# Keeping the last expert's rows on chip and adding them with TensorE

## The chip, the cores and the metric

The kernel runs on one core of a Trainium2 chip. The metric is the device time of one execution in microseconds (us). The core's engines are named as the profile names them: PE is TensorE (PEld its weight loads), ACT is ScalarE, DVE is VectorE, POOL is GpSimd, and SP is SyncE, which here issues most of the loads. Each engine works through its own queue of instructions in order; DMA queues move data between device memory (DRAM tensors, names ending in `_d`) and the chip. PSUM is the memory that TensorE writes into, 8 banks of 128 rows by 512 fp32 numbers.

## The reference, cut to what matters

The program computes two transformer blocks on 1024 tokens of width 1024. The first ends in a mixture of experts; the second begins with a norm of the result and a projection. In between:

```python
# end of block 1: x_tok [1024 tokens, 1024], 16 experts, each takes its 128 best tokens
logits = x_tok @ w_router;  aff = softmax(logits)
g, idx = top_k(aff.T, 128)                       # gate and token index of each expert's rows
xs = x_tok[idx]                                  # [16, 128, 1024]
y = (silu(xs @ w_gate) * (xs @ w_up)) @ w_down * g[..., None]
ff = zeros([1024, 1024]).at[idx].add(y)          # a token may be taken by several experts
h = h + g2 * rmsnorm(ff, norm_post_ffn)
# start of block 2
u = rmsnorm(h, norm_w)
proj = u @ w_in                                  # 8 column groups, then the HGRN and the
...                                              # forgetting-attention branches, output, final norm
```

Products are made in about fp32 precision: each factor is split into a high and a low part (type fp32r) and three products hi·hi, hi·lo and lo·hi are summed (`mm3`, L78 to L84).

## The kernel before, in words

**Order of the work.** The functions issue operations in program order into a tile framework. A planner then puts each engine's operations into one fixed queue, by the times at which it expects them to be ready; among ready ones, program order decides. Memory on chip and PSUM are handed out in pools, stacked and opened and closed by the program; a tile of a later pool may lie on the bytes of an earlier one, and then waits for the last use of the tiles it lies on.

**The experts (`moe`, L679).** The loop runs 17 times. Pass e multiplies the 128 rows of expert e by its gate and up weights (`rows` into the PSUM tiles pg and pu) and, in the same pass, expert e-1's hidden rows by its down weights (py). Weights come in pieces of 1 MB: SP loads a piece into one of 6 slots `raw` (L535), ACT casts it to `whi` (L87), and DVE takes the difference to `wlo` (L88). At the end of a pass ACT applies silu (L713, tile `sl`), DVE multiplies by pu (L714, tile `hh`), and `combine` (L772) finishes expert e-1: ACT multiplies py by the gate into `y` (L776), and POOL issues an indirect DMA (L777) that adds the 128 rows of y at their tokens into `ff_d` in device memory. `chosen` fetches the next expert's rows `xs` by an indirect DMA. The last pass, e = 16, holds only the down product and combine of expert 15.

**Block 1's end and block 2's start (`ffn_out`, L793).** For each of 8 blocks of 128 tokens SP loads the residual `h` (L803) and the experts' sum `ff` (L805), 512 KB each. ACT squares ff with a running sum (L808), the reciprocal root comes from a logarithm and an exponential (L92, L93), DVE scales ff (L810) and adds it to h (L811); h is stored, squared again (L813), and its reciprocal root is put on a diagonal `dg` (L816). After each 4 blocks (a group), for each of 8 column slices k, TensorE multiplies h by dg, which transposes and scales (L822, PSUM tile `tp`, 2 buffers); ACT makes `uh` (L824) and DVE `ul` (L825), the split transposed input of block 2.

**What follows (`hgrn`).** `wk` (L828) loads the first columns of block 2's weights, `raw` with 2 buffers (load L835, 512 KB in 512-byte pieces), and splits them; `chan` (L863) multiplies them with uh and ul into PSUM tiles `mm`, by L82 to L84. The mm and the tp tiles belong to one PSUM pool, `b2p` (L789), which holds both `ffn_out` and `hgrn`. `hgrn` reads its `masks` last at L1058 and ends with transposes (L1139) and stores (L1141, L1181). Then the attention stage opens pools on the same bytes and banks; its first load on SP, `cmask` (L1196), reads an input of the program.

Of the kernel before, what the change touches and what calls it, by code (L numbers as in the profile page):

```python
# [40 lines left out]
def f(ap):  # L41
    return ap.bitcast(F32)
# [7 lines left out]
class Kernel:  # L50
# [628 lines left out]
    def moe(self):  # L679

        with ExitStack() as st:
# [3 lines left out]
            pp = self.pool(st, "moep", 1, space=PSUM)  # L685
            xs = self.chosen(0, w, pp)
            hh = None
            for e in range(NE + 1):
# [20 lines left out]
                if e < NE:  # L709
                    hh = self.t(w, [P, D], F32, "hh", bufs=2)  # L710
                    for n in range(2):
                        sl = self.t(w, [P, 512], F32, "sl", bufs=2)
                        self.silu = self.nc.scalar.activation(sl, pg[n], AF.Silu)  # L713
                        self.nc.vector.tensor_tensor(hh[:, n * 512:(n + 1) * 512], sl, pu[n], op=ALU.mult)  # L714
                if e:
                    self.combine(e - 1, w, py)
        self.stx.close()
# [53 lines left out]

    def combine(self, e, w, py):  # L772

        y = self.t(w, [P, D], F32, "y", bufs=2)
# [5 lines left out]
    def block2(self):  # L780
        with ExitStack() as st:
            self.stu = ExitStack()
            up = self.pool(self.stu, "uT", side="right")
            self.u = [(self.t(up, [P, KB, 512], F32R, f"uh{g}"), self.t(up, [P, KB, 512], F32R, f"ul{g}")) for g in range(2)]
            self.pj = self.pool(st, "pj")
            self.jobs, self.ready = [], []
            with ExitStack() as st2:
                self.pp = self.pool(st2, "b2p", 2, space=PSUM)
                self.ffn_out()  # L789
                self.hgrn()  # L790
            self.fox()

    def ffn_out(self):  # L793

        nc, pp = self.nc, self.pp
        with ExitStack() as st:
            w = self.pool(st, "fo")
            for g in range(2):
                us = []
                for b in range(4):  # L800
                    r = slice((g * 4 + b) * P, (g * 4 + b + 1) * P)
                    h = self.t(w, [P, D], F32, "h", bufs=8)
                    nc.sync.dma_start(h, self.h_d[r, :])  # L803
                    ff = self.t(w, [P, D], F32, "ff", bufs=4)
                    nc.sync.dma_start(ff, self.ff_d[r, :])  # L805
                    sq = self.t(w, [P, D], F32, "sq", bufs=2)
                    ss = self.t(w, [P, 2], F32, "ss", bufs=4)
                    nc.scalar.activation(sq, ff, AF.Square, accum_out=ss[:, 0:1])  # L808
                    self.rstd(ss[:, 0:1], D)
                    nc.vector.scalar_tensor_tensor(ff, ff, ss[:, 0:1], self.G2, op0=ALU.mult, op1=ALU.mult)  # L810
# [4 lines left out]
                    dg = self.t(w, [P, P], F32, "dg", bufs=8)  # L815
                    nc.vector.tensor_scalar(dg, self.ident, ss[:, 1:2], None, op0=ALU.mult)  # L816
                    us.append((h, dg))
                uh, ul = self.u[g]
                for k in range(KB):
                    tp = self.t(pp, [P, 512], F32, "tp", bufs=2)  # L820
# [3 lines left out]
                    nc.scalar.activation(uh[:, k, :], tp, AF.Copy, scale=nw)  # L824
                    nc.vector.scalar_tensor_tensor(ul[:, k, :], tp, nw, f(uh[:, k, :]), op0=ALU.mult, op1=ALU.subtract)  # L825
# [36 lines left out]

    def chan(self, ws, g, m=P):  # L863

        ps = self.t(self.pp, [P, 512], F32, "mm", bufs=self.nmm)
        x = self.u[g]
        self.mm3(ps[:m, :], [(ws[k], (x[0][:, k, :], x[1][:, k, :])) for k in range(KB)])
        return ps

    def toks(self, ws, b):  # L870

        ps = self.t(self.pp, [P, 512], F32, "mm", bufs=self.nmm)
        for j in range(2):
            x, t0 = self.u[(b + j) // 4], ((b + j) % 4) * P
            self.mm3(ps[:, j * 256:(j + 1) * 256], [((x[0][:, k, t0:t0 + P], x[1][:, k, t0:t0 + P]), ws[k]) for k in range(KB)])
# [614 lines left out]
def shape_constants():  # L1490
# [14 lines left out]
        "k_ident": np.eye(P, dtype=np.float32),  # L1505
        "k_cos": np.ascontiguousarray(np.concatenate([cos, cos], 0)),
# [28 lines left out]
```

## Time and profile before

| | us |
|---|---|
| median of 3 runs (lowest, highest) | 2838.47 (2833.11, 2840.96) |
| the profiled execution | 2839.24 |
| its span | 2837.3 |
| idle of PE between the last expert and block 2 | 24.65 |
| the last expert's scatter, start to landing | 10.50 |

The profiled execution is one run with the hardware profiler on; its span is the time from its first to its last instruction, and all stretches below are microseconds from the start of that span. Mean granted clock of TensorE over the span: 0.966 of full. In a timeline row the columns are start, duration, engine and line, operation with output<-input, shapes and how many in a row; in brackets the idle time of the engine before it and what ended it. A chain of waits follows the work that ended last backwards, each piece with its start, duration and engine.

### The profile page before, as it was taken

The page shows a single profiled execution, that of the slowest core. Times are in us where ns is not written, and L with a number is a line of the kernel's source. Part 1 is how long each engine was busy: PE and PEld are TensorE (multiplying, and loading weights), DVE is VectorE, ACT ScalarE, POOL GpSimd, SP SyncE. Part 2 cuts the span into 40 slices and gives each one's busy share as a digit, 9 for nine tenths or more (in the row PEclk, how much of TensorE's full clock was granted, in tenths as well). Part 3 has the DMA queues.
Part 4 walks back from the last instruction along what each step waited for, and adds up shares of the span by engine and source line. Part 5 has one row for each costly group of instructions (what it writes and reads, how often), then busy time and mean ns, then how long its engine had stood idle before and what let it go on. Part 6 is the DMA issues. An engine that isn't in the chain of part 4 may idle for free.

```text
span 2837.3 us, 38733 instructions
## 1 busy us (share of the span) xinstructions
PE 2638.5 (93%) x14237; PEld 2221.2 (78%) x14237; DVE 1995.0 (70%) x3298; ACT 1620.8 (57%) x2858; POOL 247.6 (9%) x355
## 2 busy tenths in 40 slices
PE   6999999899799999997699999998999998989998
PEld 3777888777588877776589999997878787777886
DVE  5965899844798888886656777763777676786535
ACT  4212898833477777775644555543666665674335
POOL 0101000000300000000100000000111111230000
PEclk8999999999899999999799999999999999999999
DMA  7665332256599999997612122336665666465612
GB/s 274 221 229 191 102 91 88 86 178 211 216 390 381 366 370 375 377 362 234 233 39 46 45 46 38 46 81 164 175 166 133 156 163 135 141 194 188 207 60 82
DMA packets 306018, 516.44 MB, mean 182 GB/s; under 512 B 52529, under 2 KB 180094, under 8 KB 304804
## 3 DMA queue, kind: packets, MB, share of 16 engines
q1 hardware_dynamic: 288556, 456.04, 50.8%
q0 software_dynamic: 11136, 36.25, 4.3%
q10 hardware_dynamic: 6136, 21.67, 2.0%
q8 instruction: 113, 1.85, 0.3%
q14 instruction: 77, 0.63, 0.1%
HBM read 421.01 MB, written 92.88 MB: 181 GB/s over the span
## 4 chain that ended last, share of the span: by engine, by line
PE 72%; DMA 10%; ACT 8%; DVE 6%; issue 3%; SPq 1%; POOL 0%; DVEq 0%; ACTq 0%; POOLq 0%
PE mm L82 13%; PE mm L84 12%; PE mm L83 12%; PE av L1333 2%; PE pu L763 2%; PE pu L764 2%; PE pu L762 2%; PE py L764 2%; PE py L763 2%; PE py L762 2%; PE pg L763 2%; PE pg L764 2%; PE sc L1052 2%; PE pg L762 2%; PE tp L1324 1%
## 5 line engine op out<-in xcount | busy, mean ns | idle before, releaser
L88 DVE TENSOR_TENSOR wlo<-raw,whi 128x2048 fp32r<-128x2048 f32 (+1 forms) x280 | 541.9, 1963 | 172.2 <-ACT whi L87 167.6
L87 ACT CAST whi<-raw 128x2048 fp32r<-128x2048 f32 (+1 forms) x284 | 459.6, 1656 | 137.1 <-PE mm L83 63.8
L82 PE MATMUL mm<-uh,whi 128*128 128x512 f32 x640 | 257.9, 403 | 0.9 <-ACT uh L824 0.9
L83 PE MATMUL mm<-ul,whi 128*128 128x512 f32 x640 | 255.0, 398 | 0.0
L84 PE MATMUL mm<-uh,wlo 128*128 128x512 f32 x640 | 254.4, 398 | 0.0
L84 PE MATMUL mm<-whi,ul 128*128 128x256 f32 x768 | 221.5, 288 | 0.0
L82 PE MATMUL mm<-whi,uh 128*128 128x256 f32 x768 | 221.1, 288 | 0.0
L83 PE MATMUL mm<-wlo,uh 128*128 128x256 f32 x768 | 218.8, 285 | 0.0
L84 PEld LDWEIGHTS mm<-whi,ul 128*128 128x128 f32 x768 | 148.1, 193 | 0.1
L82 PEld LDWEIGHTS mm<-whi,uh 128*128 128x128 f32 x768 | 148.0, 193 | 0.2
L83 PEld LDWEIGHTS mm<-wlo,uh 128*128 128x128 f32 x768 | 147.9, 193 | 0.2
L1302 ACT ACTIVATE lg<-lg,sm 128x128 f32<-128x128 f32 (+7 forms) x128 | 99.5, 777 | 80.4 <-DVE sm L1301 79.7
L84 PEld LDWEIGHTS mm<-uh,wlo 128*128 128x128 f32 x640 | 122.6, 192 | 24.4
L82 PEld LDWEIGHTS mm<-uh,whi 128*128 128x128 f32 x640 | 122.8, 192 | 23.3 <-ACT uh L824 1.4
L446 ACT ACTIVATE e<-sc,mx 128x512 f32<-128x512 f32 (+1 forms) x192 | 117.8, 624 | 40.4 <-DVE mx L445 39.6
L83 PEld LDWEIGHTS mm<-ul,whi 128*128 128x128 f32 x640 | 122.7, 192 | 22.0
L1333 PE MATMUL av<-pT,V 128*128 128x256 f32 x640 | 110.2, 300 | 19.8 <-ACT pT L87 15.1
L82 PE MATMUL mm<-xh,whi 128*128 128x512 f32 x320 | 126.8, 396 | 1.4 <-DVE cy L520 1.0
L84 PE MATMUL mm<-xh,wlo 128*128 128x512 f32 x320 | 126.4, 396 | 0.5 <-DVE wlo L88 0.5
L1333 PEld LDWEIGHTS av<-pT,V 128*128 128x128 f32 x640 | 93.3, 198 | 42.8 <-ACT pT L87 31.9
L83 PE MATMUL mm<-xl,whi 128*128 128x512 f32 x320 | 126.5, 395 | 0.0
L1298 DVE SCALAR_TENSOR_TENSOR lg<-sc,FT,nF 128x512 f32<-128x512 f32 (+3 forms) x160 | 91.7, 583 | 37.8 <-PE sc L1295 27.0
(392 smaller groups left out, 7002.1 us busy)
## 6 DMA issues: line engine op xcount, KB each, us to landing
raw<-in_w_gate_dram SPq DMA_DIRECT2D x64, 1024.0 KB
raw<-in_w_up_dram SPq DMA_DIRECT2D x64, 1024.0 KB
raw<-in_w_down_dram SPq DMA_DIRECT2D x64, 1024.0 KB
raw<-in_w_in_dram SPq DMA_DIRECT2D x76, 512.0 KB
wada<-in_w_ada_dram SPq DMA_DIRECT2D x32, 512.0 KB
Q<-Q_d SPq DMA_DIRECT2D x64, 256.0 KB
yraw<-yT_d SPq DMA_DIRECT2D x22, 512.0 KB
wa<-in_w_ada_dram SPq DMA_DIRECT2D x8, 1024.0 KB
```

The lines of the kernel that those rows point to most:

```text
L82: self.nc.tensor.matmul(ps, ah, bh, start=(i == 0), stop=False)
L83: self.nc.tensor.matmul(ps, ah, bl, start=False, stop=False)
L84: self.nc.tensor.matmul(ps, al, bh, start=False, stop=(i == n - 1))
L87: self.nc.scalar.copy(hi, src)
L88: (eng or self.nc.vector).tensor_tensor(lo, src, f(hi), op=ALU.subtract)
L446: nc.scalar.activation(e[:, c0:c0 + n], ps[:, :n], AF.Exp, scale=-1.0, bias=mx[:, m, c:c + 1], accum_out=sm[:, m, c:c + 1])
L762: self.nc.tensor.matmul(ps[n], xh[:, i, :], hi[:, k, c], start=(i == 0), stop=False)
L763: self.nc.tensor.matmul(ps[n], xh[:, i, :], lo[:, k, c], start=False, stop=False)
L764: self.nc.tensor.matmul(ps[n], xl[:, i, :], hi[:, k, c], start=False, stop=(i == KB - 1))
L1298: nc.vector.scalar_tensor_tensor(lg[:, c0:c0 + full], ps[:, :full], Ft, nF[:, c0:c0 + full], op0=ALU.subtract, op1=ALU.add)
L1302: nc.scalar.activation(lg[:, :n], lg[:, :n], AF.Exp, scale=-1.0, bias=sm[:, 0:1], accum_out=sm[:, 1:2])
L1333: nc.tensor.matmul(ps[:, :256], V[:, k, :], pT[k // 4][j][:, k % 4, :], start=(k + j == 0), stop=(k == nkb - 1 and j == 1))
```

## The change

The last expert (15) has no scatter any more. Its gated rows stay on chip as a high part `yh` (ACT) and a low part `yl` (DVE). While it runs, `places` builds a matrix `oh` [128 rows, 1024 tokens]: it loads a row 0..1023 on all partitions and compares it with the expert's token indices, 1 where equal. In `ffn_out` TensorE adds up, for each token block and each half of the columns, identity times ff (what the other 15 experts left in device memory) and oh times yh and yl, in PSUM; the square and the scaling read that sum. All 8 loads of h and all 8 of ff are issued ahead of the loop, into buffers of their own. `ffn_out` has a PSUM pool of its own, `fop` (the sums 3 x 2 banks, tp 2 banks: all 8), closed before `b2p` is opened for `hgrn`. uh and ul lie in the buffers that held the experts' weights (`mw`), which stays open. To make room, `hh`, `sl` and `y` have one buffer instead of two.

```diff
@@ -683,6 +683,11 @@
             self.pad(st, 64)
             self.ml = self.pool(st, "ml", 2)
             pp = self.pool(st, "moep", 1, space=PSUM)
+            self.stl = ExitStack()
+            lp = self.pool(self.stl, "last", side="right")
+            self.yh, self.yl = [self.t(lp, [P, D], F32R, x) for x in ("yh", "yl")]
+            self.oh = self.t(lp, [P, SEQ], F32R, "oh")
+            self.ix = self.t(lp, [P, 1], F32, "ix")
             xs = self.chosen(0, w, pp)
             hh = None
             for e in range(NE + 1):
@@ -707,14 +712,22 @@
                     for q in range(4):
                         self.rows(py, hT, q)
                 if e < NE:
-                    hh = self.t(w, [P, D], F32, "hh", bufs=2)
+                    hh = self.t(w, [P, D], F32, "hh", bufs=1)
                     for n in range(2):
-                        sl = self.t(w, [P, 512], F32, "sl", bufs=2)
+                        sl = self.t(w, [P, 512], F32, "sl", bufs=1)
                         self.silu = self.nc.scalar.activation(sl, pg[n], AF.Silu)
                         self.nc.vector.tensor_tensor(hh[:, n * 512:(n + 1) * 512], sl, pu[n], op=ALU.mult)
-                if e:
+                if e == NE - 1:
+                    self.places(e, w)
+                if e == NE:
+                    gate = self.gT[:, e - 1:e]
+                    for n in range(2):
+                        c = slice(n * 512, (n + 1) * 512)
+                        self.nc.scalar.activation(self.yh[:, c], py[n], AF.Copy, scale=gate)
+                        self.nc.vector.scalar_tensor_tensor(self.yl[:, c], py[n], gate, f(self.yh[:, c]), op0=ALU.mult, op1=ALU.subtract)
+                elif e:
                     self.combine(e - 1, w, py)
-        self.stx.close()
+        self.stu = self.stx
 
     def tsplit(self, pp, w, src, nblk, name, bufs=2):
 
@@ -769,9 +782,17 @@
         self.nc.gpsimd.indirect_dma_start(out=xs, out_offset=None, in_=self.xn2_d, in_offset=bass.IndirectOffsetOnAxis(ap=self.idxT[:, e:e + 1], axis=0))
         return self.tsplit(pp, w, xs, KB, "xs", bufs=2)
 
+    def places(self, e, w):
+
+        nc = self.nc
+        at = self.t(w, [P, D], F32, "xs", bufs=2)
+        nc.sync.dma_start(at, rowbc(self.I["k_iota"]))
+        nc.vector.tensor_copy(self.ix, self.idxT[:, e:e + 1])
+        nc.vector.tensor_scalar(self.oh, at, self.ix, None, op0=ALU.is_equal)
+
     def combine(self, e, w, py):
 
-        y = self.t(w, [P, D], F32, "y", bufs=2)
+        y = self.t(w, [P, D], F32, "y", bufs=1)
         for n in range(2):
             self.nc.scalar.activation(y[:, n * 512:(n + 1) * 512], py[n], AF.Copy, scale=self.gT[:, e:e + 1])
         self.nc.gpsimd.indirect_dma_start(out=self.ff_d, out_offset=bass.IndirectOffsetOnAxis(ap=self.idxT[:, e:e + 1], axis=0), in_=y, in_offset=None, compute_op=ALU.add)
@@ -779,50 +800,60 @@
 
     def block2(self):
         with ExitStack() as st:
-            self.stu = ExitStack()
-            up = self.pool(self.stu, "uT", side="right")
-            self.u = [(self.t(up, [P, KB, 512], F32R, f"uh{g}"), self.t(up, [P, KB, 512], F32R, f"ul{g}")) for g in range(2)]
+            self.u = [[[self.t(self.mw, [P, 4, 512], F32R, n) for _ in range(2)] for n in ("whi", "wlo")] for g in range(2)]
             self.pj = self.pool(st, "pj")
             self.jobs, self.ready = [], []
+            self.ffn_out()
+            self.stl.close()
             with ExitStack() as st2:
                 self.pp = self.pool(st2, "b2p", 2, space=PSUM)
-                self.ffn_out()
                 self.hgrn()
             self.fox()
 
     def ffn_out(self):
 
-        nc, pp = self.nc, self.pp
+        nc = self.nc
         with ExitStack() as st:
             w = self.pool(st, "fo")
+            pp = self.pool(st, "fop", 2, space=PSUM)
+            small = [[self.t(w, [P, D], F32, "sq", bufs=2), self.t(w, [P, P], F32, "dg", bufs=8)]]
+            hs = [self.t(w, [P, D], F32, *x) for x in [("h", 6)] * 6 + [("hl", 2)] * 2]
+            for b in range(8):
+                nc.sync.dma_start(hs[b], self.h_d[b * P:(b + 1) * P, :])
+            ffs = [self.t(w, [P, D], F32, "ff", bufs=8) for _ in range(8)]
+            for b in range(8):
+                nc.sync.dma_start(ffs[b], self.ff_d[b * P:(b + 1) * P, :])
             for g in range(2):
                 us = []
-                for b in range(4):
-                    r = slice((g * 4 + b) * P, (g * 4 + b + 1) * P)
-                    h = self.t(w, [P, D], F32, "h", bufs=8)
-                    nc.sync.dma_start(h, self.h_d[r, :])
-                    ff = self.t(w, [P, D], F32, "ff", bufs=4)
-                    nc.sync.dma_start(ff, self.ff_d[r, :])
-                    sq = self.t(w, [P, D], F32, "sq", bufs=2)
+                for b in range(g * 4, g * 4 + 4):
+                    r = slice(b * P, (b + 1) * P)
+                    h, ff = hs[b], ffs[b]
+
+                    ps = self.t(pp, [P, D], F32, "ff", bufs=3)
+                    for n in range(2):
+                        c = slice(n * 512, (n + 1) * 512)
+                        nc.tensor.matmul(ps[:, c], self.ident, ff[:, c], start=True, stop=False)
+                        nc.tensor.matmul(ps[:, c], self.oh[:, r], self.yh[:, c], start=False, stop=False)
+                        nc.tensor.matmul(ps[:, c], self.oh[:, r], self.yl[:, c], start=False, stop=True)
+                    sq, dg = small.pop() if small else (self.t(w, [P, D], F32, "sq", bufs=2), self.t(w, [P, P], F32, "dg", bufs=8))
                     ss = self.t(w, [P, 2], F32, "ss", bufs=4)
-                    nc.scalar.activation(sq, ff, AF.Square, accum_out=ss[:, 0:1])
+                    nc.scalar.activation(sq, ps, AF.Square, accum_out=ss[:, 0:1])
                     self.rstd(ss[:, 0:1], D)
-                    nc.vector.scalar_tensor_tensor(ff, ff, ss[:, 0:1], self.G2, op0=ALU.mult, op1=ALU.mult)
+                    nc.vector.scalar_tensor_tensor(ff, ps, ss[:, 0:1], self.G2, op0=ALU.mult, op1=ALU.mult)
                     nc.vector.tensor_tensor(h, h, ff, op=ALU.add)
                     self.store(self.h2_d[r, :], h)
                     nc.scalar.activation(sq, h, AF.Square, accum_out=ss[:, 1:2])
                     self.rstd(ss[:, 1:2], D)
-                    dg = self.t(w, [P, P], F32, "dg", bufs=8)
                     nc.vector.tensor_scalar(dg, self.ident, ss[:, 1:2], None, op0=ALU.mult)
                     us.append((h, dg))
-                uh, ul = self.u[g]
                 for k in range(KB):
+                    uh, ul = self.uk(g, k)
                     tp = self.t(pp, [P, 512], F32, "tp", bufs=2)
                     for b, (h, dg) in enumerate(us):
                         nc.tensor.matmul(tp[:, b * P:(b + 1) * P], h[:, k * P:(k + 1) * P], dg, start=True, stop=True)
                     nw = self.VC[:, 40 + k:41 + k]
-                    nc.scalar.activation(uh[:, k, :], tp, AF.Copy, scale=nw)
-                    nc.vector.scalar_tensor_tensor(ul[:, k, :], tp, nw, f(uh[:, k, :]), op0=ALU.mult, op1=ALU.subtract)
+                    nc.scalar.activation(uh, tp, AF.Copy, scale=nw)
+                    nc.vector.scalar_tensor_tensor(ul, tp, nw, f(uh), op0=ALU.mult, op1=ALU.subtract)
 
 
     def wk(self, c0, n):
@@ -860,19 +891,22 @@
             ws = self.wk(c0, n)
             self.ready += [(u, ws) for u in units]
 
+    def uk(self, g, k, c=slice(None)):
+
+        return [x[k // 4][:, k % 4, c] for x in self.u[g]]
+
     def chan(self, ws, g, m=P):
 
         ps = self.t(self.pp, [P, 512], F32, "mm", bufs=self.nmm)
-        x = self.u[g]
-        self.mm3(ps[:m, :], [(ws[k], (x[0][:, k, :], x[1][:, k, :])) for k in range(KB)])
+        self.mm3(ps[:m, :], [(ws[k], self.uk(g, k)) for k in range(KB)])
         return ps
...
+        "k_iota": np.arange(SEQ, dtype=np.float32)[None, :],
```

## Rows read from the trace of the kernel before

**Rows 1.** The page, part 1: busy time, share of the span, instructions.
```profile
PE 2638.5 (93%) x14237; PEld 2221.2 (78%) x14237; DVE 1995.0 (70%) x3298; ACT 1620.8 (57%) x2858; POOL 247.6 (9%) x355
```

**Rows 2.** Stretches: length, busy PE, PEld, DVE, ACT, POOL, granted clock, DMA share, GB/s.
```profile
1353.60:1372.90 19.30, 4.51 (x16) 3.66 (x16) 13.16 (x14) 15.67 (x42) 2.79 (x5) 0.50 1.02 409
1372.90:1400.50 27.60, 25.63 (x154) 22.18 (x154) 18.74 (x26) 18.22 (x40) 2.43 (x4) 0.89 0.38 148
1400.50:1450.00 49.50, 49.50 (x320) 40.54 (x320) 20.62 (x35) 17.73 (x33) 6.05 (x10) 1.00 0.33 87
...
1356.00:1358.00 2.00, 0.00 (x0) 0.00 (x0) 1.88 (x2) 1.20 (x3) 0.00 (x0) 0.50 1.03 424
```

**Rows 3.** Timeline of PE: last products of the experts, first of block 2.
```profile
1329.83 0.40 PE L763 MATMUL py<-wlo,hth 128*128 128x512 f32 x1
...
1336.18 0.39 PE L764 MATMUL py<-whi,htl 128*128 128x512 f32 x1
1361.23 1.19 PE L822 MATMUL tp<-dg,h 128*128 128x128 f32 x4 [24.65 <-DVE dg L816]
```

**Rows 4.** Chain of waits, the pieces around that gap: start, us, what.
```profile
1337.57 10.50 DMA ff_d<-y,idxT
1348.17 5.38 DMA ff<-ff_d
1353.63 1.16 ACT sq L808 x2
```

**Rows 5.** Timeline of SP's queue in the gap.
```profile
1332.94 11.38 SPq L835 DMA_DIRECT2D raw<-in_w_in_dram  x3
1344.43 0.60 SPq L803 DMA_DIRECT2D h<-h_d  x1
```

**Rows 6.** Timeline of ACT: casts of block 2's first weights; last uh.
```profile
1345.61 1.04 ACT L87 CAST whi<-raw 128x1024 fp32r<-128x1024 f32 x1 [2.94 <-DMA raw<-in_w_in_dram]
1351.10 1.04 ACT L87 CAST whi<-raw 128x1024 fp32r<-128x1024 f32 x1 [4.44 <-DMA raw<-in_w_in_dram]
...
1399.81 0.69 ACT L824 ACTIVATE uh<-tp,VC 128x512 fp32r<-128x512 f32 x1 [0.21 <-PE tp L822]
```

**Rows 7.** Timeline of PE: sixteen records of plain fp32 products, and the next.
```profile
1379.92 1.95 PE L822 MATMUL tp<-dg,h 128*128 128x128 f32 x16
1381.62 0.48 PE L83 MATMUL mm<-ul,whi 128*128 128x512 f32 x1
```

**Rows 8.** Stretches of the mm tile alone: length, PE, PEld, DVE, ACT, clock, DMA, GB/s.
```profile
1372.90:1380.00 7.10, 2.97 (x7) 1.87 (x7) 0.00 (x0) 0.00 (x0) 0.56 1.03 393
1380.00:1390.00 10.00, 4.97 (x18) 2.98 (x17) 0.00 (x0) 0.00 (x0) 1.00 0.26 107
1390.00:1400.50 10.50, 4.51 (x16) 2.89 (x17) 0.00 (x0) 0.10 (x1) 1.00 0.06 23
```

**Rows 9.** Timelines of DVE, PE and SP where hgrn hands over to attention.
```profile
1926.35 0.90 DVE L1058 COPY_PREDICATED ST<-masks,sc 128x256 f32<-128x256 uint8 x2
...
1947.44 1.01 PE L1139 MATMUL tp<-ident,t 128*128 128x128 f32 x4 [2.62 <-DVE t L1133]
...
1950.44 0.32 SPq L1181 DMA_DIRECT2D G_d<-sth  x1
1950.86 0.39 SPq L1196 DMA_DIRECT2D cmask<-in_k_cmask_dram  x1
```

**Rows 10.** Timeline of DVE: one difference of 512 columns, one sum of 1024.
```profile
1356.69 1.23 DVE L811 TENSOR_TENSOR h<-h,ff 128x1024 f32<-128x1024 f32 x1
...
1378.93 0.75 DVE L825 SCALAR_TENSOR_TENSOR ul<-tp,VC,uh 128x512 fp32r<-128x512 f32 x1 [0.75 <-ACT uh L824]
```

**Rows 11.** Timelines of ACT and DVE within a pass; ACT's waits, 800 to 1300.
```profile
1228.96 7.34 ACT L87 CAST whi<-raw 128x2048 fp32r<-128x2048 f32 x4
...
1235.06 1.37 DVE L714 TENSOR_TENSOR hh<-sl,pu 128x512 f32<-128x512 f32 x2 [1.07 <-PE pu L764]
...
ACT y L776 <- PE py L764: 84.1, 12, 8.8
```

More of the change, by code (lines that the diff above doesn't have):

```diff
@@ L873, in toks @@
         for j in range(2):
-            x, t0 = self.u[(b + j) // 4], ((b + j) % 4) * P
-            self.mm3(ps[:, j * 256:(j + 1) * 256], [((x[0][:, k, t0:t0 + P], x[1][:, k, t0:t0 + P]), ws[k]) for k in range(KB)])
+            g, t0 = (b + j) // 4, ((b + j) % 4) * P
+            self.mm3(ps[:, j * 256:(j + 1) * 256], [(self.uk(g, k, slice(t0, t0 + P)), ws[k]) for k in range(KB)])
         return ps.rearrange("p (b c) -> p b c", b=2)
```

## The prediction

> **What bounds the kernel now.** I read the page first: TensorE is busy for 93% of the span [rows 1]. So an edit pays only where TensorE stands still, and the stretches around the change show where that is. From 1400.50 on, PE is busy for all of 49.50 us; between 1353.60 and 1372.90 it is busy for 4.51 of 19.30 us, and from 1372.90 to 1400.50 for 25.63 of 27.60 [rows 2]. The timeline of PE gives the hole itself: the last product of the experts starts at 1336.18 and runs 0.39 us, so they end at 1336.57, and the first product of block 2 starts at 1361.23, after 24.65 us [rows 3]. The chain of waits through the hole is the last expert's scatter, 10.50 us from 1337.57, then the load of ff, 5.38 us from 1348.17, then the first square on ACT at 1353.63 [rows 4]. By the chain alone, taking the scatter away would be worth some 10 us.
>
> SP's queue tells another story. Its three loads of block 2's weights start at 1332.94 and hold the queue for 11.38 us, to 1344.3, because the third waits for one of two raw buffers; the first h follows at 1344.43 [rows 5]. ACT casts the second raw at 1345.61 and the third at 1351.10, each as soon as it has landed [rows 6]. So the rows of h and ff stand in line behind weights that are slow to arrive, and with the scatter gone that line is still there.
>
> The end of the stage is the last uh, at 1399.81 + 0.69 = 1400.5 [rows 6]. Any delay of it pushes a PE that is full afterwards [rows 2], so delays here count one for one.
>
> **The change part by part.**
>
> *The scatter goes.* That frees the ff loads from 1348.07 (its end) to whatever is late next: the loads' own line. When does ff of block 0 land? All h and ff loads are now issued first in program order, 8 of h and then 8 of ff, so one ff is behind eight h: nine loads of 512 KB. In the row of 1356 to 1358 the DMA moves 424 GB/s [rows 2], so a load takes 524288 / 424e3 = 1.24 us, nine take 11.1.
> By the Trainium skill, page "DMA: Bandwidth & Descriptors", section "Where 436 GB/s comes from", the memory side binds at about 358 GB/s for such loads, which would make a load 1.46 us and the nine 13.2, an estimate that would put 2 us on the sum; the 424 GB/s of [rows 2] decides against it.
>
> Where the nine start depends on the order of SP's queue. Can they start while the last expert runs? Their pool lies on bytes that the experts' raw and xs tiles had, which were free early, and h_d was written long before. Yet in the kernel before, h of block 0 needs no scatter either and comes only at 1344.43, behind three weight loads that stand after it in the program [rows 5]. The handover from hgrn to attention shows the same: the mask's last reader is at 1926.35, and cmask, which depends on no computed data, is issued only at 1950.86, behind that stage's last store at 1950.44 [rows 9]. I take from both that the planner lets a new pool's operations in only when the old pool is over, even if the tiles waited for on the chip are free. So I expect SP to issue two raw loads, then eight h, then ff, and none of them during the last expert's products. Bounds for the landing of ff 0: if two raws and nine rows run at full rate from the issue of the first raw, 1332.94 [rows 5], 11 x 1.24 = 13.6 gives 1346.5; if the nine follow the second raw, cast at 1345.61 [rows 6], 1345.6 + 11.1 = 1356.8. If the third raw also goes ahead of them, 1351.1 + 11.1 = 1362.2. I take 1353, above the middle of the first two, because raws come slowly (the second and the third were cast 5.5 us apart, [rows 6]): 0.6 us earlier than the 1353.55 before (1348.17 + 5.38, [rows 4]). The later ff come each 1.24 us after, faster than the squares use them.
>
> *Placing the rows on TensorE.* For each block and half: one plain fp32 product of 512 columns and two fp32r ones. Sixteen fp32 records (8 products of 128 columns) take 1381.62 - 1379.92 = 1.70 us at full clock [rows 7], so a product of 512 columns takes 4 x 1.70 / 8 = 0.85. An fp32r product takes (1336.18 - 1329.83) / 28 = 0.227 us [rows 3]. A block is 2 x 0.85 + 4 x 0.227 = 2.6 us at full clock, 5.2 at half. After the idle hole the granted clock is 0.50, half [rows 2], and the hole is still there, so block 0 costs 5.2, and with 0.2 for the hand-over ACT squares at 1353 + 5.4 = 1358.4: +4.8 on the path. Seven more blocks lie beside ACT, which does 15.67 us of work in 19.30 [rows 2] and sets the pace at about 4.2 us a block; at half clock 5.2 is over that pace by 1.0, so up to three slow blocks add 0 to 3. I take 0, as PE is now loaded sooner and may be granted its full clock sooner.
> By the Trainium skill, page "TensorE: Matmul & The Clock Gate", section "Loop structure matters more than you think", a long wait for a transfer ahead of matmuls leaves the engine cold; by that rule all four blocks of the first group would be placed at half clock, which is the +3 end of that term.
>
> *From the first square to the last uh.* Before: 1400.5 - 1353.6 = 46.9 us. The same squares, roots, sums and splits remain on ACT and DVE, reading PSUM instead of memory on chip for two of them; I take 46.9 again, hence 1405.3 for the last uh.
>
> *The overlap with block 2's first products.* In the kernel before, PE does 7 + 18 + 16 = 41 products of mm between 1372.90 and 1400.50 [rows 8], in the gaps of `ffn_out`: 41 x 0.227 = 9.3 us of work at full clock. Now `ffn_out` has all 8 banks of PSUM in its own pool, and mm gets its banks from a pool opened after that is closed. On the chip a mm tile need only wait for the tile that lay on its bank. But the handover from hgrn shows what the planner makes of it: PE stands 2.62 us before the transpose at 1947.44 [rows 9], with block 2's next products not drawn into that gap. So I expect none of the 41 before the last uh, and 9.3 us come back behind it. (Bounds: 0 if the overlap stays whole, 9.3 if it goes.) The third raw and its split move behind too, but two raws and their splits are there to start with.
>
> *The rows themselves.* yh and yl replace y: ACT as before, DVE 2 x 0.75 [rows 10], all done by about 1338.8, long before 1353: nothing. `places`: one 512 KB load, a copy, and a comparison over 1024 columns, bounded by 0 and by 1.23 us + a copy, the sum of the same size [rows 10]. It is on DVE within the last full pass, which waits at times [rows 11]. I take 0.5.
>
> *Single buffers.* y is free a whole pass before it is written again, hh is read a pass earlier: nothing; and ACT has 84.1 us of idle in 12 passes just ahead of y [rows 11]. sl is the sharp one: silu of the second half now waits until DVE has multiplied the first, which is when pu is complete (1235.06) [rows 11]. ACT runs four casts at that time, to 1236.30; if the second silu is planned behind the fourth, it finds hh done and costs nothing. I take 0 (the other case is a rival).
>
> **The sum**: -0.6 + 5.4 = +4.8 for the first square, +9.3 for the lost overlap, +0.5 for `places`: +14.6. On the profiled execution, 2839.24 (its span 2837.3 and 1.9 around it), that is 2853.8; that execution lies 0.8 above the median, so 2853.
>
> **The rivals.**
> (F) *The loads run ahead and the overlap stays.* If h lands during the last expert and ff right after expert 14's scatter, only y is late: yl at 1338.3, two fp32r products, square at 1338.8 instead of 1353.63: -14.8, 2824. For it: per-tile waits, bytes free early, an idle DMA before 1334; against it: the order of SP's queue in [rows 5] and [rows 9]. If the data are early and the overlap is lost, -14.8 + 9.3 = -5.5: 2833, which is no change here.
> (S) *Loads as I expect, overlap kept.* +4.8 + 0.5: 2844, also no change. For it: PSUM waits on the chip are per tile, and the sums' banks come free after block 7; against it: PE's gap in [rows 9].
> (K) *The single sl stalls every pass.* If the second silu stands one cast earlier in ACT's queue, ACT waits for hh (1235.75) and 0.64 of silu instead of going to the fourth cast, which would begin at 1234.46 = 1236.30 - 1.84: 1.9 us late, and with hh's second half (0.69) and a hand-over 0.3 before DVE's next difference 2.9; DVE's wlo is what TensorE's next products need. 15 passes: +43, to 2882 alone, 2897 with the rest. For it: DVE runs differences back to back after hh; against it: the 84.1 us of ACT's slack, 7 a pass. It decides as soon as that delay passes the slack.
> That the change doesn't do what it says, h not loaded during the last expert, is part of the forecast.
>
> **How the numbers follow.** Forecast (row loads behind the weights, overlap lost) 0.50, at 2846 to 2861 (landing of ff 0 from -6.5 to +3.8, slow blocks 0 to 3, `places` 0 to 1.3; the third raw ahead of the rows would add up to 5.4 more, which gives the upper end below); K 0.10; S 0.12; early data with lost overlap 0.08; F 0.20. The bound of what can be told from no change is 0.3%, 8.5 us. Faster: F, 0.20. Same: 0.12 + 0.08 = 0.20. Slower: 0.50 + 0.10 = 0.60. The range goes from F's own value, 2824 (half of F lies below), to 2866, and leaves out K: 0.10 + 0.10.
>
> **What would show it.** In the trace after: SP's first h after the second raw, near 1334, and no h load during the last expert (else F); the first square near 1358; the granted clock 0.50 over the first placements of block 0; no mm product before the last uh (else S); the last uh near 1405, and PE full from there; unchanged pass lengths of the experts (else K). A first square before 1345 would make the prediction wrong, whatever the total.

## The result and the profile after

The kernel after takes 2861.27 us (median of 4 runs, 2856.84 to 2862.48), the one before beside it 2835.79: ratio 1.0079, 95% interval 1.0064 to 1.0094, so slower by 18 to 27 us. The forecast was 2853, slower, with 2824 to 2866 as its range.

The stretches of the profiled execution after (columns as in [rows 2]): from the experts' end (the last py's start plus 0.39) to the first square, from there to the last uh, and on. Before, the first two were 17.1 and 46.9 us long [rows 3, 4, 6].

```profile
1335.10:1362.80 27.70, 4.37 (x9) 2.59 (x10) 3.86 (x4) 2.82 (x5) 0.00 (x0) 0.57 0.92 331
1362.80:1410.90 48.10, 40.23 (x188) 28.94 (x187) 33.28 (x41) 34.55 (x83) 5.07 (x9) 0.89 0.38 135
1410.90:1450.00 39.10, 39.10 (x245) 35.47 (x244) 14.37 (x26) 11.87 (x22) 7.01 (x10) 1.00 0.24 68
```

So the first square is 10.6 us later, and the stage behind it 1.2 longer. SP's queue shows the first part: two weight loads, eight rows of h (`hl` are the last two), and only then ff, as the forecast had it. The first h is issued at 1333.22, 1.9 us before the experts' end, and none earlier ([rows 5] had three weight loads and then rows in turn).

```profile
1332.12 0.99 SPq L866 DMA_DIRECT2D raw<-in_w_in_dram  x2
1333.22 10.99 SPq L822 DMA_DIRECT2D h<-h_d  x6
1344.32 3.08 SPq L822 DMA_DIRECT2D hl<-h_d  x2
1348.38 8.96 SPq L825 DMA_DIRECT2D ff<-ff_d  x8
1358.36 15.51 SPq L866 DMA_DIRECT2D raw<-in_w_in_dram  x3
...
1970.89 0.41 SPq L1230 DMA_DIRECT2D cmask<-in_k_cmask_dram  x1
```

The eight loads of ff are not issued at once: SP holds each until one more row of h has landed, and so they stand some 1.24 us apart. First two of them alone, then SP's waits at that line (us in total, times, the longest):

```profile
1350.78 0.32 SPq L825 DMA_DIRECT2D ff<-ff_d  x1
1352.03 0.32 SPq L825 DMA_DIRECT2D ff<-ff_d  x1
```
```profile
SPq L825 <- DMA h<-h_d: 5.4, 6, 1.0
```

PE's timeline: the first placement waits for ff until 1358.43, and the first product of block 2's projection is behind the last transposes. The transposes at 1396.70, after 3.07 us of idle, run at half clock (four records in 1.22 us), the last ones at full clock again (0.61):

```profile
1334.71 0.39 PE L777 MATMUL py<-whi,htl 128*128 128x512 f32 x1
1358.43 2.04 PE L835 MATMUL ff<-ff,ident 128*128 128x512 f32 x2 [23.33 <-DMA ff<-ff_d]
...
1396.70 1.22 PE L853 MATMUL tp<-dg,hl 128*128 128x128 f32 x4 [3.07 <-DVE dg L847]
...
1409.55 0.61 PE L853 MATMUL tp<-dg,hl 128*128 128x128 f32 x4
1409.91 0.47 PE L82 MATMUL mm<-whi,whi 128*128 128x512 f32 x1
```

The handover to attention (the cmask load, last row of SP's fence; 1950.86 before, [rows 9]) is a good mark, because the experts' end itself moves by some us from execution to execution: experts' end to cmask is 614.3 us before and 635.8 after, +21.5. Of that 10.6 + 1.2 lie before the last uh, and 9.7 behind it. From the last uh to cmask, before and then after:

```profile
1400.50:1950.86 550.36, 544.08 (x3713) 496.75 (x3713) 368.50 (x735) 274.99 (x558) 7.50 (x17) 1.00 0.27 55
```
```profile
1410.88:1970.89 560.01, 551.39 (x3745) 502.68 (x3744) 369.55 (x735) 275.48 (x558) 8.49 (x17) 1.00 0.26 53
```
So 7.3 of the 9.7 are more work of PE, the products that no longer overlap, and 2.3 are more idle time of it. (The span differs by only 17.8, since the experts ended 1.5 earlier in this execution and attention took 2.2 less; it was also the fastest of the four runs.)

### The profile page after: what moved, and what is told of

The parts are those of the page before. It is cut to its first block, busy times and chain, and to the rows that moved or that the text cites. A ratio compares the mean times of both kernels' runs of the same rounds, so it can differ in the third digit from the quotient of the medians.

```text
span 2855.1 us, 38903 instructions
## 1 busy us (share of the span) xinstructions
PE 2653.9 (93%) x14301; PEld 2227.2 (78%) x14301; DVE 1997.9 (70%) x3302; ACT 1619.7 (57%) x2858; POOL 246.0 (9%) x354
## 4 chain that ended last, share of the span: by engine, by line
PE 54%; DMA 8%; ACT 6%; DVE 3%; issue 1%; POOL 0%; SPq 0%; DVEq 0%; ACTq 0%; POOLq 0%
PE mm L82 9%; PE mm L84 9%; PE mm L83 9%; PE av L1367 2%; PE pu L777 2%; PE pu L776 2%; PE pu L775 2%; PE py L777 2%; PE py L776 2%; PE py L775 2%; PE pg L776 2%; PE pg L777 2%; PE sc L1086 2%; PE pg L775 2%; DMA Q_d<-stl 1%
## 5 line engine op out<-in xcount | busy, mean ns | idle before, releaser
L82 PE MATMUL mm<-whi,whi 128*128 128x256 f32 (+1 forms) x1408 | 477.5, 339 | 0.8 <-ACT yo L1174 0.8
L84 PE MATMUL mm<-whi,wlo 128*128 128x256 f32 (+1 forms) x1408 | 475.0, 337 | 0.0
L83 PE MATMUL mm<-wlo,whi 128*128 128x256 f32 (+1 forms) x1408 | 471.9, 335 | 0.0
L84 PEld LDWEIGHTS mm<-whi,wlo 128*128 128x128 f32 x1408 | 269.4, 191 | 24.5
L82 PEld LDWEIGHTS mm<-whi,whi 128*128 128x128 f32 x1408 | 269.5, 191 | 23.3 <-ACT yo L1174 1.0
L83 PEld LDWEIGHTS mm<-wlo,whi 128*128 128x128 f32 x1408 | 269.4, 191 | 22.4
L445 DVE TENSOR_REDUCE mx<-sc 128x1 f32<-128x512 f32 (+1 forms) x192 | 110.1, 593 | 7.6 <-PE sc L444 6.8
L776 PE MATMUL pg<-wlo,xsh 128*128 128x512 f32 x256 | 101.5, 397 | 10.0 <-DVE wlo L88 10.0
L1329 PE MATMUL sc<-K,Q 128*128 128x512 f32 (+2 forms) x384 | 102.3, 377 | 8.6 <-DVE lg L1334 5.6
L88 DVE TENSOR_TENSOR pT<-tp,pT 128x512 fp32r<-128x512 f32 (+1 forms) x192 | 102.5, 549 | 10.2 <-ACT pT L87 9.2
```

The costliest lines, as they stand in the source:

```text
L82: self.nc.tensor.matmul(ps, ah, bh, start=(i == 0), stop=False)
L83: self.nc.tensor.matmul(ps, ah, bl, start=False, stop=False)
L84: self.nc.tensor.matmul(ps, al, bh, start=False, stop=(i == n - 1))
L88: (eng or self.nc.vector).tensor_tensor(lo, src, f(hi), op=ALU.subtract)
L445: nc.vector.tensor_reduce(mx[:, m, c:c + 1], ps[:, :n], axis=AX.X, op=ALU.min)
L776: self.nc.tensor.matmul(ps[n], xh[:, i, :], lo[:, k, c], start=False, stop=False)
```

## The experiments

All marks in the table are in us. E is the experts' end; the ratio is to the kernel before on the same chip.

| run | ratio (95%) | E to first square | to last uh | E to cmask |
|---|---|---|---|---|
| before | | 17.1 | 46.9 | 614.3 |
| after | 1.0079 (1.0064, 1.0094) | 27.7 | 48.1 | 635.8 |
| e1_own_banks | 1.0037 (1.0023, 1.0051) | 17.1 | 49.5 | 623.8 |
| e2_interleaved | 1.0042 (1.0028, 1.0056) | 17.0 | 47.3 | 625.7 |
| e3_single_buffers | 0.9991 (0.9980, 1.0003) | 16.6 | 48.2 | 615.7 |
| e4_no_last_scatter | 1.0007 (0.9996, 1.0018) | 13.6 | 53.4 | 614.7 |
| e5_no_placement | 1.0057 (1.0039, 1.0074) | 22.8 | 48.4 | 628.1 |
| e6_order_and_overlap | 1.0032 (1.0021, 1.0042) | 15.9 | 54.5 | 622.5 |
| e8_early_rows | 1.0073 (1.0055, 1.0092) | 4.3 | 55.6 | 611.4 |
| e9_early_rows_scatter | 1.0123 (1.0103, 1.0144) | 12.2 | 60.1 | 622.2 |
| e10_order_and_banks | 1.0009 (1.0000, 1.0018) | 18.9 | 46.8 | 615.1 |
| e11_early_in_weight_slots | 1.0010 (1.0001, 1.0019) | 9.5 | 46.2 | 603.4 |
| e12_early_and_ordered | 0.9976 (0.9967, 0.9986) | 2.8 | 54.9 | 608.7 |
| e13_casts_later | 0.9941 (0.9928, 0.9955) | 2.8 | 47.4 | 598.1 |

In e8, e9 and e11 E itself comes 10 to 11 us later than in the kernel before (1347.7, 1346.6 and 1346.9 against 1336.6). The marks, which start at E, don't hold that.

**Does a PSUM pool of its own cost the overlap?**

```diff
 # before
+            self.ffn_out()                      # with pp = self.pool(st, "fop", 2, space=PSUM)
             with ExitStack() as st2:
                 self.pp = self.pool(st2, "b2p", 2, space=PSUM)
-                self.ffn_out()
                 self.hgrn()
```


> The kernel before, with one edit: ffn_out's tp tiles get a PSUM pool of their own, closed before b2p is opened. Theory (the planner lets hgrn's products in only when ffn_out's pool is over): none of the 41 mm products before the last uh, first square unchanged at about 17 us after the experts' end, last uh unchanged, whole time +9.3 us over the kernel before. Rival (a tile waits only for the tile on its own bank, so the overlap stays): +0 to 2 us, mm products in the gaps of ffn_out as before.

Measured +10 us (2850.40 against 2840.19), and 9.5 up to cmask. No mm stands before the last transposes. The stretches of this run, and behind them the second one in the kernel before:

```profile
1337.80:1354.90 17.10, 0.00 (x0) 0.00 (x0) 3.68 (x3) 3.82 (x5) 1.54 (x1) 0.66 0.83 206
1354.90:1404.40 49.50, 26.18 (x131) 22.76 (x132) 32.06 (x40) 33.89 (x81) 5.25 (x9) 0.67 0.61 241
```
```profile
1353.60:1400.50 46.90, 30.14 (x168) 25.84 (x169) 31.89 (x40) 33.89 (x81) 5.22 (x9) 0.73 0.64 255
```
The stage is 2.6 longer as well. PE has less to do in it, and the granted clock is 0.67 instead of 0.73; that this is what made it longer was not tested by itself. So 6.8 of the 9.5 lie behind the last uh.

What keeps mm out, e1 alone does not settle. PE, the first mm:

```profile
1403.83 0.50 PE L82 MATMUL mm<-uh,whi 128*128 128x512 f32 x1 [0.19 <-DVE ul L826]
```
It reads inputs of the first group, which were done long before, and yet waits for a ul of the second, an operation that reads a tp. So its bank seems to have been one of tp's two, and the chip held it as well. The kernel after speaks for the order of the queue: there six of fop's eight banks held the sums, DVE read the last of them until 1395.19, PE then stood idle for over a microsecond more than once, and the first mm came only at 1409.91. DVE of the kernel after, the last reading of a sum:

```profile
1393.91 1.28 DVE L842 SCALAR_TENSOR_TENSOR ff<-ff,ss,G 128x1024 f32<-128x1024 f32 x1
```

**Does the line of row loads set the first square?**

```diff
 # after
+            ffs = [...]                         # allocated ahead
             for b in range(8):
+                nc.sync.dma_start(ffs[b], self.ff_d[b * P:(b + 1) * P, :])
                 nc.sync.dma_start(hs[b], self.h_d[b * P:(b + 1) * P, :])
-            ... (the loop of the eight ff)
```


> The kernel after, with the loads issued ff0, h0, ff1, h1, ... instead of eight h and then eight ff. Theory (ff of block 0 lands late because it is the ninth row load in a line of 1.24 us each): it is now the first after the two raw loads, so the first square comes 8 x 1.24 = 9.9 us earlier than in the kernel after, less up to 1.5 for a start still behind the raws; whole time -8 to -10 us against the kernel after, some 2852. Rival (the two raw loads or TensorE's placement set the start, not the row loads ahead of ff): no change, 2861.

2850.07, 10 to 11 us under the kernel after; the first square is 10.7 us earlier. The eight h ahead of the first ff cost just that: in the kernel after the second weight load was cast at 1347.09, and 9 x 1.24 behind that is 1358.3, where the placement began; here it was cast at 1344.89, and the placement began 1.4 us behind it, at 1346.25.

**Was the scatter what held the stage?**

```diff
 # before
-                    self.combine(e - 1, w, py)
+                    self.combine(e - 1, w, py, e < NE)   # last call: y, but no indirect DMA
```


> The kernel before without the last expert's scatter (expert 15's rows are left out of the sum); nothing else. Reading by the chain of waits alone: the scatter's 10.5 us go, first square 10 us earlier, 2826. Theory (the row loads stand in SP's line behind the weight loads): ff0 lands two row loads after the second raw, about 1348, so the first square is 5 us earlier and the time -5 us against the kernel before, 2831.

No gain, neither the 10.5 us of the chain's reading nor my 5. The first square is 3.5 us earlier, and the stage behind it 6.5 longer: without the scatter the planner put the third weight load behind all rows, and its cast early on ACT. SP, then ACT of this run:

```profile
1370.21 0.32 SPq L806 DMA_DIRECT2D ff<-ff_d  x1
1370.62 15.94 SPq L836 DMA_DIRECT2D raw<-in_w_in_dram  x3
```
```profile
1383.87 1.05 ACT L87 CAST whi<-raw 128x1024 fp32r<-128x1024 f32 x1 [2.76 <-DMA raw<-in_w_in_dram]
```
ACT stands 2.76 us at that cast with uh's work behind it, PE runs dry and its granted clock over the stage is 0.69 (0.73 before). A gain was given back within 30 us by a wait that the chain of the kernel before could not show.

**Single buffers, and the placement, each alone.**

```diff
 # before: hh, sl, y            # after: squares read ff
-  bufs=2                       -  ps = self.t(pp, [P, D], F32, "ff", bufs=3)  and six products
+  bufs=1                       +  ps = ff
```


> The kernel before with one buffer instead of two for hh, sl and y, nothing else. Theory (the second silu finds hh done, the scatter and hh are a pass old): pass lengths unchanged, +0 us, within 3. Rival (ACT waits for hh's first half in every pass, with four casts behind it): up to +43 us.

> The kernel after without the placement: TensorE puts nothing in place and the squares read ff from its buffer (expert 15's rows are left out of the sum). Theory (block 0's placement at half clock stands on the path, the others lie beside ACT): the first square 4.4 us earlier after ff 0's landing, time -4 to -5 us against the kernel after. Rival (placements of all blocks hold the squares back): -10 us or more. Other rival (the placements keep TensorE's clock up and pay for themselves): 0 or slower.

Single buffers cost nothing measurable. The wait that the rival named is there in every pass of the kernel after (ACT's timeline, second silu):

```profile
1224.88 0.60 ACT L718 ACTIVATE sl<-pg 128x512 f32<-128x512 f32 x1 [1.53 <-PE pg L777]
1236.54 0.60 ACT L718 ACTIVATE sl<-pg 128x512 f32<-128x512 f32 x1 [3.83 <-DVE hh L719]
1261.38 0.60 ACT L718 ACTIVATE sl<-pg 128x512 f32<-128x512 f32 x1 [1.52 <-PE pg L777]
```
But from pass to pass it is 36.5 us (1261.38 - 1224.88), as before: the 3.83 come out of the slack ahead of y [rows 11], of which some 5 us are left. ACT before, and then after:

```profile
1246.88 0.69 ACT L776 ACTIVATE y<-py,gT 128x512 f32<-128x512 f32 x1 [8.09 <-PE py L764]
```
```profile
1247.63 0.69 ACT L797 ACTIVATE y<-py,gT 128x512 f32<-128x512 f32 x1 [5.07 <-PE py L777]
```
The placement left out brings the first square 4.9 us forward, with a ratio of 1.0057 instead of 1.0079, and leaves the stage as it was (48.4 against 48.1): up to the last uh its price is block 0's alone, as forecast. Another 3.1 us that e5 gains from there to cmask are not explained.

**Overlap given back, twice.** First with the sums in halves in b2p's banks, then with full sums and mm and tp in a pool opened before:

```diff
 # e6: e2, with                        # e10: e2, with
+ ffn_out inside b2p                   + pool A (2 mm, 2 tp) opened ahead of ffn_out
+ ps = two 512-column tiles (sc, o, mm)+ sums: 2 buffers of 2 banks in pool B
+ two squares, an add, two scalings    + sc, o, a third mm: pool C behind B
```


> The kernel after with the interleaved loads, and with ffn_out inside b2p again: the sums are made in halves in the banks of sc, o and mm, squared in halves. Theory: -9 us for the loads and -9.3 for the overlap, +1 to 3 for twice as many squares and their sum, against the kernel after: about 2845, still 5 to 10 above the kernel before, because two raws and a placement are still ahead of the first square. Rival (the overlap costs as much as it gives because the placements fill TensorE's gaps): about 2852.

> The kernel after with interleaved loads (ff first) and the overlap given back without halving the sums: mm (two tiles) and tp in a PSUM pool opened before ffn_out, the sums in two buffers of two banks, and a pool for sc, o and a third mm tile opened behind it. Theory: first square 16 to 17 us after the experts' end as in the interleaved run, stage from first square to last uh 47 to 50 us, some 40 mm products in it, so -8 to -10 us against the interleaved run, about the time of the kernel before (0 to +3). Rival (in the run with halves it was not the halving but TensorE's sums and mm together that made the stage longer): stage 53 us or more, -2 to -4 us against the interleaved run.

e6 missed its expectation: -2 us against e2, because its stage is 54.5 us long; it has 16 ACT instructions more than e10 (98 against 82). e10 rules out that rival (sums and mm together on TensorE): 46.8 us with 37 mm products in it, and a time 8 us under e2 (2841.89). That leaves the halving, or the sums' place in banks of sc, o and mm; e6 changed both at once. Their stages, e6 and then e10:

```profile
1350.90:1405.30 54.40, 48.14 (x228) 35.46 (x228) 34.96 (x57) 35.15 (x98) 5.02 (x9) 0.93 0.57 212
```
```profile
1355.40:1402.30 46.90, 44.65 (x232) 32.92 (x231) 33.13 (x41) 35.15 (x82) 5.07 (x9) 1.00 0.61 222
```
With both losses mended the change is level with the kernel before: no scatter, and a placement at half clock in its place.

**Can the rows really come while the last expert runs?** They need a pool that is open then. First try: the experts' weight slots.

```diff
 # e8: e10, with
+ rf = rawrows(h_d[256 rows]) x4, rawrows(ff_d[256 rows]) x2    # pool "raws"
+ "last" pool below w; pj on the right; w_out_2's blocks in mw's buffers
 # e9: e8 with the scatter, no placement
```


> The kernel after with three things mended: h and the first half of ff are loaded into the experts' own weight slots (the pool is open, so the planner can issue them while the last expert runs; pj moves to the right side and w_out_2's blocks take mw's buffers); block 2's first two mm tiles and tp lie in a PSUM pool opened before ffn_out and the sums in two buffers of their own; the third mm, sc and o in a pool behind it. Theory: h and ff are there when the last rows are ready, the first square comes some 5 us after the experts' end (17 before, 28 after) with TensorE still at full clock, some 40 mm products stay in ffn_out's gaps, and the stage from first square to last uh is 47 to 50 us: -9 to -12 us against the kernel before, some 2829. Rival (ffn_out is bound by ACT and DVE and by what is planned behind it, so an earlier start is given back): 0.

> As the run with early rows, but the last expert is scattered as in the kernel before and nothing is placed: only h is loaded early, ff waits for the scatter; tp and mm in b2p as before. Theory: ff 0 lands one load after the scatter, so the first square comes some 12.5 to 13 us after the experts' end, 4.5 earlier than before: -3 to -5 us, unless the weights, which now stand behind ff in SP's queue, come too late for mm: then 0.

The first square came 4.3 us after E, as expected, and yet e8 is slower than the kernel before. Three things took it back. First, the experts' passes became 37.0 us long instead of 36.5, which is 8 of the 11 us by which E moved, to 1347.7: the records of most of TensorE's products there are 6 ns longer, as the rows of one group show, before and then e8 (min/median/max ns):

```profile
L763 PE MATMUL pu<-wlo,xsh x176: 387/389/486, 900.2 to 1299.5; 128*128 128x512 f32 x176
```
```profile
L779 PE MATMUL pu<-wlo,xsh x176: 392/395/397, 905.5 to 1282.8; 128*128 128x512 f32 x176
```
The small pool below w shifts the addresses of all that the experts read. That this is the cause was not separated from the other moves of e8, but with that pool back in its place (e11) a pass is 36.5 again. Second, behind cmask e8 loses 11 us more (897.7 to the span's end, 886.4 before), where w_out_2's blocks moved; that was not separated either. Third, the stage is 55.6 long, as ACT waits 3.53 and 1.60 us for the weights that now stand behind the rows. e9's first square is where it was expected (12.2), but its weights stand behind an ff that waits for the scatter: stage 60.1. Its time missed the expectation by far, 33 us over the kernel before: E comes 10 us later as in e8, cmask 7.9 later behind E, and another 14 are lost behind cmask. These two say nothing for or against early rows as such.

**The version that beats both.** Rows of blocks 0 to 3 go into mw's buffers, which block 2's second group needs last; pools as in the kernel after and e10.

```diff
 # e11: e10, with
+ whi x2 <- h_d (2 x 256 rows), wlo x2 <- ff_d, taken from mw in pass 15
 # e12: taken in pass 16, behind the last expert's own blocks; and
+ issue_after: weight loads 3, 4 behind the rows; casts behind the squares of blocks 1, 2, 5
 # e13: casts behind the squares of blocks 3, 5, 6
```


> The same banks, and h and ff of blocks 0 to 3 loaded into the weight buffers (mw) that block 2's first-group inputs don't need yet, so that the planner can issue them in the open pool, ahead of the weights of block 2; the rows of blocks 4 to 7 follow behind those weights; the experts' memory lies as in the kernel before. Theory: first square 4 to 5 us after the experts' end (17 before), stage 48 to 51 us, last uh some 53 to 56 us after the experts' end (64 before), 40 mm products kept: -7 to -11 us against the kernel before, some 2831. Rival (given back: the rows of blocks 4 to 7 or the weights come late, and ACT and TensorE wait for them inside the stage): 0 or less than 3 us faster.

e11: no gain. From E to cmask it is 10.9 us shorter than before, but E comes 10.3 later. The order taken from the pools hurt twice. Its four tiles took the slots that the last expert's weights were to have, so that PE stood 7.03 us in the last expert's products; and ACT had the casts of block 2 queued ahead of the last expert's rows (timelines of PE and ACT):

```profile
1329.78 1.22 PE L782 MATMUL py<-whi,hth 128*128 128x512 f32 x2 [7.03 <-ACT whi L87]
```
```profile
1342.87 1.05 ACT L87 CAST whi<-raw 128x1024 fp32r<-128x1024 f32 x1 [11.34 <-DMA raw<-in_w_in_dram]
1345.33 1.05 ACT L87 CAST whi<-raw 128x1024 fp32r<-128x1024 f32 x1 [1.42 <-DMA raw<-in_w_in_dram]
1350.01 1.04 ACT L87 CAST whi<-raw 128x1024 fp32r<-128x1024 f32 x1 [3.63 <-DMA raw<-in_w_in_dram]
1350.96 1.26 ACT L729 ACTIVATE yh<-py,gT 128x512 fp32r<-128x512 f32 x2
```


> The run with rows in the weight slots, with its two faults mended: the four tiles for h and ff of blocks 0 to 3 are taken after the last expert's own weight blocks, so that those get their slots in turn; and the first casts of block 2's weights are held on ACT's queue behind squares of blocks 1, 2 and 5, their loads behind the rows of blocks 4 to 7, so that ACT never stands at a cast ahead of the last expert's rows. Theory: experts' end where it was, first square 4 to 6 us after it (17 before), stage 47 to 50 us, last uh 52 to 56 us after the experts' end (64 before), some 40 mm products kept: -7 to -11 us against the kernel before, some 2830. Rival (something in the stage takes it back once more, as in the two early runs before this one): within 3 us of the kernel before.

e12: -6.8 us, just under the range expected (7 to 11). First square 2.8 us after E, but the stage is 54.9: ACT stands at the first cast, PE then runs dry and comes back at half clock. ACT, then PE of e12:

```profile
1355.09 1.04 ACT L87 CAST whi<-raw 128x1024 fp32r<-128x1024 f32 x1 [3.57 <-DMA raw<-in_w_in_dram]
```
```profile
1359.03 1.23 PE L862 MATMUL tp<-dg,whi 128*128 128x128 f32 x4 [4.21 <-DVE dg L856]
1360.60 0.80 PE L82 MATMUL mm<-whi,whi 128*128 128x512 f32 x1 [0.35 <-ACT whi L864]
```


> The run before this one with one thing moved: the casts of block 2's first weights are held behind squares of blocks 3, 5 and 6 instead of 1, 2 and 5. There ACT stood 3.57 us at the first cast for a load that had not landed, and TensorE was idle for 4.21 us behind it and fell to half clock. Theory (that stall is what the stage still gives back): no wait over 1 us at that cast, stage from first square to last uh 50 to 52 us instead of 54.9, last uh some 54 us after the experts' end: another -3 to -4 us, about -10 against the kernel before. Rival (ACT's work only moves, and DVE's or the tail of the last blocks sets the end): within 1 us of that run.

e13: 2823.66 us, ratio 0.9941, 13 to 20 us faster than the kernel before. More than expected: not only the 3.57 us went (0.86 is left), the granted clock is 1.00 from E to the end of the stage, which is 47.4 long:

```profile
1332.70:1335.50 2.80, 2.80 (x9) 1.44 (x9) 1.41 (x2) 0.72 (x3) 0.00 (x0) 1.00 1.03 420
1335.50:1382.90 47.40, 45.08 (x230) 32.59 (x229) 35.30 (x43) 36.71 (x84) 5.05 (x9) 1.00 0.68 226
1382.90:1450.00 67.10, 66.90 (x471) 57.93 (x470) 35.56 (x61) 26.78 (x46) 6.75 (x11) 1.00 0.22 57
```
ACT, the first cast of this run:

```profile
1352.30 1.04 ACT L87 CAST whi<-raw 128x1024 fp32r<-128x1024 f32 x1 [0.86 <-DMA raw<-in_w_in_dram]
```
The early rows are issued while the last expert still runs (E is 1332.69 here). SP:

```profile
1316.21 3.08 SPq L730 DMA_DIRECT2D whi<-h_d  x2
1326.52 0.87 SPq L730 DMA_DIRECT2D wlo<-ff_d  x2
```
From E to the last uh it is 50.2 us instead of 63.9; another 2.4 up to cmask are not explained.

## Why the prediction was right, and where it was off

*The order of SP's queue*: right. Two weight loads, eight h, eight ff, the first of them 3 us before the experts' end and none earlier. The reason given for it (a new pool's operations enter the queues only when the pool under it is over) is borne out by e11 to e13, which get rows early by taking them from a pool that is open. e1 loses the overlap by a pool alone, but there the banks may have held mm as well.

*The landing of ff 0*: the mis-sized term. I took 1353, 16.4 us after E; it was 1358.4, 23.3 after E, outside the two bounds that I weighed (1346.5 and 1356.8) though not outside the third, 1362.2. The right working was the upper one: nine rows landed one by one, 1.24 us apart, behind the second weight load (SP's waits and e2 show it), and that was cast 1.5 us later than in the kernel before, 3.0 later counted from E (why wasn't tried). I had moved down from that bound as if rows and weights ran side by side. In part they did: from 1334 to 1348 the DMA moved 3.1 MB, and the two weight loads are 1.0 of it; but no row landed sooner for it.

*The load's size*: 512 KB in 1.24 us held; from 1348 to 1358 the DMA moved 416 to 422 GB/s in each 2 us. The Trainium skill's 358 ("DMA: Bandwidth & Descriptors", "Where 436 GB/s comes from") is not what binds here.

*The placement on the path*: 5.4 forecast, 4.4 measured (1358.43 to 1362.80), since the clock came back within block 0: it is 0.50 from 1358 to 1360, and then

```profile
1360.00:1362.00 2.00, 2.00 (x6) 1.19 (x4) 0.00 (x0) 0.00 (x0) 0.00 (x0) 0.64 1.03 419
1362.00:1364.00 2.00, 2.00 (x8) 1.21 (x7) 0.00 (x0) 1.17 (x3) 0.00 (x0) 1.00 1.06 385
```
e5 gives 4.9. Later blocks are placed at full clock and lie beside ACT, as forecast; the +3 end of the term, all four blocks of the group at half clock, did not come.

*The first square to the last uh*: 46.9 taken, 48.1 measured.

*The lost overlap*: 9.3 forecast, all of it work of PE behind the last uh. Of the 9.7 found there only 7.3 are work and 2.3 are idle time, which the forecast did not have; e1 has 6.8 there and 2.6 in the stage ahead of it. That the totals agree so well is in part luck.

*`places` and single buffers*: 0.5 and 0 forecast; passes and E unchanged, e3 within 0.3%. Rival K's wait exists (3.83 us a pass), its price does not.

Sum: +14.6 forecast, +21.5 up to cmask measured. The difference, 6.9, is as large as the miss of the landing; the small ones (placement -1.0, stage +1.2, overlap +0.4, `places` -0.5) nearly cancel. Rival F (faster) failed on its condition: it asked for the first square 2.2 us after E with the overlap kept, at -14.8. e12 and e13 make both happen, with the square 2.8 after E, and have -6.8 and -18 (2823.66 against 2841.78): the price could be had, but only with the casts out of the way too.

By the Trainium skill, "TensorE: Matmul & The Clock Gate", "Loop structure matters more than you think", a wait for transfers ahead of matmuls leaves the engine cold. The runs agree: granted clock 0.57 from E to the first square after, 1.00 in e13, where no such wait is left. But what the prediction worked out from it, half clock for all four blocks, did not follow: the clock was 1.00 from 1362 on.

## What to carry to other kernels

A transfer at the head of a chain of waits is worth only what the next late thing leaves: look at what else stands in the same queue, and in the queue's order, before counting it. Where a planner orders the queues, opening or closing a pool is an edit of the order; work that is to cross a stage's border must live in a pool that is open on both sides. And an in-order engine pays for anything queued too early: the last 10 us of this case came from moving the first casts behind work that was ready.

## What the runs showed of the hardware

The DMA moved far less while loads in 512-byte pieces were under way: in the kernel after 118 to 281 GB/s in each 2 us from 1334 to 1348, while the weights came with rows beside them, and 416 to 422 from 1348 to 1358, with rows alone. That the pieces are the cause was not tried by itself.

The same products of the experts took 389 ns in the records before and 395 in e8 and e9, 0.5 us a pass. The kernel after has 389 too, so the change itself is not what did it. In e8 and e9 several pools lie elsewhere on the chip; that this is the cause was not tried by itself.
